# A two-layer GELU network on one core: the x sums placed earlier, the w1 forms of block 1 spread out, a w1 ring with places given out as they come free, and twice the warm-up products

## The chip, the core and the metric

The kernel runs on one core of a Trainium2 chip. The core has five engines that work side by side, each through its own queue and in the order of the program: TensorE (PE in the profile; its weight loads are listed apart as PEld), VectorE (DVE), ScalarE (ACT), GpSimd (POOL) and SyncE (SP). POOL and SP are used here mostly to issue DMA transfers; each issues its transfers in program order, and a transfer whose inputs are not ready holds up all that stand behind it in that queue. Matrix products land in PSUM, which has eight banks; the other engines read them from there.

The metric is the device time of one execution in microseconds (us); less is better. The median of three runs of the kernel before is 904.36 us (903.43 to 904.62).

## The reference

```python
# x: 16 x 512 x 768, w1: 768 x 3072, b1: 3072, w2: 3072 x 768, all float32
y = np.matmul(x, w1) + b1
y = 0.5 * y * (1.0 + erf(y / np.sqrt(2.0)))
return np.matmul(y, w2).astype(np.float32)
```

So 8192 rows of x go through a 768 to 3072 layer with bias and GELU, and then through a 3072 to 768 layer.

## The kernel before

**Pairs.** The 8192 rows are taken in eleven pairs (`pairs`), p = 0 to 10. Each pair is two halves of 384 rows (`HW`), the last one two halves of 256. x is loaded as bf16 by DMA through two buffers (`xb`), turned by a DMA transpose into `xt`, and multiplied as bf16. Hidden units are handled in 24 chunks of 128 (`HC`); chunk j and chunk 12+j belong together (`HP` = 12).

**Layer 1, plain.** Pair 0, and the first three j of pair 1 (`PLAIN` = 3), use ordinary products: `plain` (line 382 for its matmul) runs six matmuls of 128x384 for one chunk and one half, then ACT applies GELU (line 136) into `g`. `first` (line 445) is the same for the first three chunks of pair 0 while x is still coming in, 128 rows at a time.

**Layer 1, seven products.** Everywhere else `product1` (line 147) makes a 2x2 block of results (two halves of rows by chunks j and 12+j) from seven products P1 to P7 instead of eight, each three matmuls. Their x operands are the raw quarters of `xt` and four sums of them in `xft`, made by `sum_x(k, w)`, k = 0 to 3, one DVE instruction each; P1 needs sum 0, P7 needs sum 3. Their w1 operands are seven *forms* per j (raw quarters and sums of them), made once by `make_w1`: one ACT copy and four DVE instructions into a staging area (`stage`: parts of the tiles `ot`, `ev`, `xft` and `st`, whichever is out of use), and a DMA that writes them to DRAM (`w1f`). From there each pair loads them again, one j at a time, through a ring of five places (`RING`, `SLOT`) in `w1t`. The ring lies over the raw w1, so a place can be filled only when all raw w1 under it has been used. `load_slot(idx)` issues the load number idx from the SP queue; it is called by P3, the last user of a place, for the load five further on.

In pair 1 and later the products are interleaved: step s runs P1 and P7 of its j, P5 of the j before, P2, P3 of the j before, P4 and P6, 21 matmuls. After P2 and P6 `fill(s)` may put one sum of the second layer into the DVE queue.

**Layer 2, fifteen products.** The 768 rows of a pair make two groups G0 and G1 of three row tiles each (pair 10 has one group and a remainder). For a group, a 3x3 block of `g` times a 3x2 block of w2 is made from fifteen products M0 to M14, each eight matmuls (line 221). Their left operands are raw blocks of `g` or sums made on DVE by `gsum` (lines 109 and 112; into `st`, or in place in `g`), their right operands are sums of w2 made once by `make_w2`. Several products accumulate one after the other in the same PSUM bank (`BANK`): bank A takes M4, M12, M10, M11 in this order, bank B takes M13, M1, M9, M0, bank C M14 and M2, bank D M8 and M3. After every product `finish2` reads the bank: the first use is an ACT copy into an output tile `ot` (line 102), M7, M6 and the rest add on DVE (line 109). So a product waits until DVE has read its bank for the product before it. The `ot` tile has four places; a finished row tile is sent to DRAM by the POOL queue (`store`).

`rest(G, m, after)` runs product m, its `finish2`, and then the listed extra work. For G0 and G1 the order is: the six products on raw blocks (M14, M8, M4, M7, M6, M13), then `middle` (M12, M2, M1, M5, M3, M10, M9, M11), then M0. `middle` puts the sum for M5 after M12, the two for M9 after M2 and the two for M0 after M1; `extra(n)` follows product n of `middle`, n = 0 to 7. Between M11 and M0 of G1 `ahead` runs P1 and P7 of the next pair's first j.

All instructions are kept in program order on each engine (`tc.keep_in_program_order`), so what the Python text issues first is also first in the queue. The lines that decide the order around the change:

```python
            rest(G1, "M14", gsums(G1, "M1"))
            rest(G1, "M8", gsums(G1, "M3b"))
            rest(G1, "M4", gsums(G1, "M10b"))
            rest(G1, "M7", [form_w1] if p == 0 else ())
...
                return [lambda: sum_x(n - 4, nxt[1])] if 4 <= n < 8 else []
            middle(G1, extra)
            if p > 0:
                ahead(p + 1)
            rest(G1, "M0")
```

**Start.** Before pair 0 the kernel runs products on a zeroed tile, `busy(8)` and, after the first x tile has been turned, `busy(5)` (line 394, 128x512 each); nothing reads their results. `turn_x0` (line 411) transposes the first x tiles on PE.

## Time and profile before

| what | us |
|---|---|
| median of three runs (lowest, highest) | 904.36 (903.43, 904.62) |
| the profiled execution: its own time | 905.5 |
| its span, first to last instruction | 903.7 |
| PE busy | 878.2 (97% of the span), 5507 matmuls |
| DVE busy | 574.7 (64%) |
| ACT busy | 397.6 (44%) |
| POOL busy | 83.7 (9%) |
| mean granted clock of TensorE | 0.992 |

The profile page gives, for one execution, the busy time of each engine, the chain of work that ended last, and groups of instructions with what ended the idle time before them. The trace behind it can be asked for a timeline (instructions in order of time, equal ones merged, with the idle time before each in square brackets and what released it), for the waits (who waited for whom, total, times, longest), and for windows (busy time of each engine in given stretches, the granted TensorE clock, the share of the DMA engines in use). Matmuls overlap by their pipeline: a 128x384 one is listed with 320 to 326 ns, but 64 in a row from 81.31 to 91.70 us are 0.1624 us apart. An idle time of PE in the listing therefore understates by 0.16 us how late a matmul starts.

### The profile page before, as it was taken

The numbers are of one execution on the slowest core, as the hardware profiler recorded it, in microseconds if no ns is written. First come the engines' busy times: TensorE is split into PE (matmuls) and PEld (weight loads), VectorE is DVE, ScalarE is ACT, GpSimd is POOL, SyncE is SP. The second block draws the span as 40 slices with busy tenths as digits, with TensorE's granted clock in tenths as the row PEclk, the third lists the DMA queues.
The fourth block names the chain that finished last, engine by engine and source line by source line (L and its number), as shares of the span: only waits on it lengthen the run. The fifth ranks groups of instructions, "written<-read, shape, count | busy, mean of one in ns | idle before, by whom it ended". The sixth has DMA issues, their size and how long they took to land.

```text
span 903.7 us, 14021 instructions
## 1 busy us (share of the span) xinstructions
PE 878.2 (97%) x5507; PEld 536.0 (59%) x5507; DVE 574.7 (64%) x1068; ACT 397.6 (44%) x790; POOL 83.7 (9%) x152
## 2 busy tenths in 40 slices
PE   8998989999999999999999999999999999999998
PEld 6665546656655665566566566655665665666774
DVE  1687756675765776566667656675765766566654
ACT  2642277137415722761473177137415712751560
POOL 6201100110011011001101000110010011000000
PEclk8999989999999999999999999999999999999999
DMA  9996596736646682666467366736646682663521
GB/s 166 207 249 131 189 340 207 147 97 215 178 90 183 201 171 77 206 197 120 139 207 165 100 192 217 136 105 211 175 88 188 211 163 75 216 191 76 190 78 70
DMA packets 89303, 148.30 MB, mean 164 GB/s; under 512 B 50812, under 2 KB 68500, under 8 KB 89236
## 3 DMA queue, kind: packets, MB, share of 16 engines
q1 hardware_dynamic: 65156, 99.02, 37.2%
q0 software_dynamic: 24080, 48.37, 24.1%
q8 instruction: 43, 0.70, 0.3%
q14 instruction: 24, 0.20, 0.1%
HBM read 124.56 MB, written 33.42 MB: 175 GB/s over the span
## 4 chain that ended last, share of the span: by engine, by line
PE 85%; DVE 10%; DMA 3%; issue 1%; ACT 1%; POOL 0%; DVEq 0%; ACTq 0%; SPq 0%; POOLq 0%
PE ps L147 41%; PE ps L221 36%; PE ps L382 5%; DVE ot L109 4%; DVE xft L109 1%; DVE st L112 1%; DMA w1f<-st 1%; DVE st L109 1%; PE ps L445 1%; DMA w1t<-in_w_dram 1%; PE ps L631 1%; DVE xft L112 1%; DVE g L112 1%; DVE g L109 1%; DMA out_dram<-ot 1%
## 5 line engine op out<-in xcount | busy, mean ns | idle before, releaser
L147 PEld LDWEIGHTS <-w1t 128*128 128x128 bf16 x2457 | 240.2, 98 | 158.1 <-issue 12.2
L147 PE MATMUL ps<-xft,w1t 128*128 128x384 bf16 (+1 forms) x1404 | 263.4, 320 | 8.3 <-DVE xft L109 8.3
L136 ACT ACTIVATE g<-ps,b1t 128x384 bf16<-128x384 f32 (+1 forms) x411 | 222.3, 570 | 88.0 <-PE ps L147 67.3
L221 PE MATMUL ps<-w2t,g 128*128 128x384 bf16 x1512 | 257.5, 326 | 1.3 <-DVE ot L109 1.3
L109 DVE TENSOR_TENSOR ot<-ot,ps 128x384 f32<-128x384 f32 x231 | 123.9, 550 | 136.8 <-ACT ot L102 100.1
L221 PEld LDWEIGHTS <-g 128*128 128x128 bf16 x1512 | 147.9, 98 | 98.9 <-issue 1.5
L147 PE MATMUL ps<-xt,w1t 128*128 128x384 bf16 (+1 forms) x1053 | 205.0, 320 | 0.7 <-DVE ps L112 0.5
L221 PE MATMUL ps<-w2t,st 128*128 128x384 bf16 x1008 | 171.0, 326 | 1.4 <-DVE st L109 0.8
L102 ACT COPY ot<-ps 128x384 f32<-128x384 f32 x128 | 58.0, 485 | 238.2 <-PE ps L221 181.7
L221 PEld LDWEIGHTS <-st 128*128 128x128 bf16 x1008 | 98.4, 98 | 67.4 <-DVE st L109 1.2
L102 ACT COPY ps<-ps 128x384 f32<-128x384 f32 (+1 forms) x117 | 52.9, 452 | 134.6 <-PE ps L147 134.4
L112 DVE TENSOR_TENSOR ev<-ps,ev 128x384 f32<-128x384 f32 (+1 forms) x117 | 63.6, 544 | 72.7 <-PE ps L147 72.0
L112 DVE TENSOR_TENSOR ps<-ps,ev 128x384 f32<-128x384 f32 (+1 forms) x117 | 64.7, 553 | 44.9 <-PE ps L147 42.9
L104 DVE COPY ev<-ps 128x384 f32<-128x384 f32 (+1 forms) x117 | 63.4, 542 | 32.1 <-PE ps L147 32.1
L79 POOL DMA_DIRECT2D xb<-in_x_dram x58 | 31.2, 542 | 487.2 <-DMA xt<-xb 485.1
L136 ACT ACTIVATE g<-ev,b1t 128x384 bf16<-128x384 f32 (+1 forms) x117 | 70.9, 606 | 11.6 <-DVE ev L112 11.5
L112 DVE TENSOR_TENSOR st<-g 128x1024 bf16<-128x1024 bf16 x107 | 72.9, 682 | 0.0
L112 DVE TENSOR_TENSOR g<-g 128x1024 bf16<-128x1024 bf16 x84 | 57.4, 683 | 0.1
L79 POOL DMA_DIRECT2D out_dram<-ot x60 | 32.6, 543 | 242.7 <-DVE ot L109 237.2
L382 PE MATMUL ps<-xt,w1t 128*128 128x384 bf16 x252 | 43.6, 335 | 6.1 <-ACT g L136 6.1
L382 PEld LDWEIGHTS <-w1t 128*128 128x128 bf16 x252 | 25.3, 100 | 23.7 <-issue 8.4
L109 DVE TENSOR_TENSOR st<-st,g 128x1024 bf16<-128x1024 bf16 x42 | 28.9, 688 | 0.7
(62 smaller groups left out, 237.4 us busy)
## 6 DMA issues: line engine op xcount, KB each, us to landing
w1t<-w1f SPq DMA_DIRECT2D x117, 672.0 KB, 4.3
out_dram<-ot POOLq DMA_DIRECT2D x60, 384.0 KB, 2.7
xb<-in_x_dram POOLq DMA_DIRECT2D x58, 192.0 KB, 3.9
w2t<-in_w_dram POOLq DMA_DIRECT2D x8, 576.0 KB, 22.5
w1t<-in_w_dram POOLq DMA_DIRECT2D x5, 576.0 KB, 21.2
w1f<-st SPq DMA_DIRECT2D x4, 672.0 KB, 9.2
w1f<-ot POOLq DMA_DIRECT2D x2, 672.0 KB, 19.6
w1f<-ot SPq DMA_DIRECT2D x2, 672.0 KB, 6.4
```

The source lines that it names most:

```text
L79: inorder(queue.dma_start(out=out, in_=in_))
L102: inorder(nc.scalar.copy(out=dst, in_=src))
L104: inorder(nc.vector.tensor_copy(out=dst, in_=src))
L109: inorder(nc.vector.tensor_tensor(out=dst, in0=a, in1=b, op=ALU.add))
L112: inorder(nc.vector.tensor_tensor(out=dst, in0=a, in1=b, op=ALU.subtract))
L136: inorder(nc.scalar.activation(out=g[:, place_h(hc), half, :w], in_=src, func=ACTF.Gelu, bias=b1t[:, hc:hc + 1], scale=sign))
L147: inorder(nc.tensor.matmul(out=ps[:, :w], lhsT=forms[:, W1F[m], kc, :], rhs=moving1(m, kc, w), start=(kc == 0 and m in ("P1", "P7")), stop ...
L221: inorder(nc.tensor.matmul(out=ps[:, :NB], lhsT=lhs[:, c, :], rhs=w2t[:, c, WF[m], :], start=(m in OPENS and c == 0), stop=(c == QC - 1), ...
L382: inorder(nc.tensor.matmul(out=py[:, :HW], lhsT=lhs[:, kc, (j % 3) * P:(j % 3 + 1) * P], rhs=xt[:, kc, half, :], start=(kc == 0), stop=(kc ...
L445: inorder(nc.tensor.matmul(out=opened[hc][:, c0:c0 + P], lhsT=w1_group(0)[:, kc, hc * P:(hc + 1) * P], rhs=xt[:, kc, half, c0:c0 + P], sta ...
L631: inorder(nc.tensor.matmul(out=ps[:, :NB], lhsT=lhs[:, c, :], rhs=w2t[:, c, WF[f], :], start=(f == terms[0][0] and c == 0), stop=(f == ter ...
```

## The change

Eight things are done, all in one file:

1. `sum_x` 0 to 3 for the next pair follow M12, M2, M1 and M5 of G1's `middle` (n = 0 to 3), where they followed M3, M10, M9 and M11 (n = 4 to 7).
2. In every pair the G1 sums M1, M3b and M10b follow M4, M7 and M6, where they followed M14, M8 and M4.
3. In pair 0 the G0 sums M1, M3b and M10b are issued ahead of the raw products, where they came after them; the five `MIDDLE` sums of G1 follow G0's M9 and M11 and G1's M14, M8 and M4, where they followed G0's M5, M3, M10, M9 and M11. The two w1 forms that pair 0 makes in G1 follow M13 and M10 (they followed M7 and M9).
4. Block 1 (pair 1) made six w1 forms and the four x sums ahead of its twelve plain products. Now forms 6, 7 and 8 come ahead of the first, second and third chunk's two plain products, the x sums behind forms 6 and 7, and forms 9, 10 and 11 are made in two halves each from `fill` in the steps s = 0, 1 and 4.
5. The staging areas of forms 8 to 11 are the two halves of `ot` in the order upper, lower, upper, lower (they were lower, upper, and the two parts of `st`).
6. The w1 ring keeps a table `where` of the place of each load. A place is given out when it comes free: places 2, 3 and 4 when the raw w1 under them has been formed, places 0 and 1 when forms 9 to 11 are done too, and from then on by P3, which passes its own place to the next load number. Before, load idx always went to place (idx + 2) mod 5, and P3 of a step issued the load five further on.
7. `raw` forms count as used once their second half has been issued (`formed`).
8. `busy(5)` becomes `busy(10)`.

```diff
@@ -113,12 +113,15 @@
 
     total = (len(pairs) - 1) * HP - PLAIN
 
+    where = {}
+
     def slot(idx):
-        s = ((idx + FIRST) % RING) * SLOT
-        return w1t[:, s:s + SLOT]
-
-    def load_slot(idx):
+        return w1t[:, where[idx] * SLOT:(where[idx] + 1) * SLOT]
+
+    def fill_slot(k):
+        idx = len(where)
         if idx < total:
+            where[idx] = k
             dma(nc.sync, out=slot(idx), in_=w1f[(idx + PLAIN) % HP, :, :])
 
     def place_h(hc):
@@ -162,7 +165,7 @@
         elif m == "P4":
             gelu1(HP + j, 0, ps, w, 1.0)
         elif m == "P3":
-            load_slot((p - 1) * HP + j - PLAIN + RING)
+            fill_slot(where[(p - 1) * HP + j - PLAIN])
             gelu1(j, 0, ps, w, 1.0)
         elif m == "P5":
             gelu1(j, 1, u, w, -1.0)
@@ -339,40 +342,46 @@
 
     made = 0
     stage = ((otf, 0), (otf, N * 4), (evf, 0), (xftf, 0), (evf, 0), (xftf, 0),
-             (stf, 0), (stf, SLOT), (otf, 0), (otf, N * 4), (stf, 0), (stf, SLOT))
+             (stf, 0), (stf, SLOT), (otf, N * 4), (otf, 0), (otf, N * 4), (otf, 0))
 
     def make_w1():
         nonlocal made
-        j = (made + PLAIN) % HP
+        n = made
+        made += 1
+        j = (n + PLAIN) % HP
         a = raw(j)
-        area, o = stage[made]
-        queue = nc.gpsimd if made < 4 else nc.sync
-        made += 1
+        area, o = stage[n]
         s = area[:, o:o + SLOT].rearrange("p (f kc c) -> p f kc c", f=7, kc=KH)
         copy("act", s[:, 0:2], a[:, 1:3])
-        add(s[:, 2], a[:, 1], a[:, 2])
-        add(s[:, 3:5], a[:, 0:4:2], a[:, 1:4:2])
-        sub(s[:, 5], a[:, 2], a[:, 0])
-        sub(s[:, 6], a[:, 1], a[:, 3])
-        dma(queue, out=w1f[j], in_=area[:, o:o + SLOT])
-
-    nload = 0
-
-    def load_raw_slots(plain_done=0):
-        nonlocal nload
-        while nload < RING:
-            k = (nload + FIRST) % RING
+
+        def one():
+            add(s[:, 2], a[:, 1], a[:, 2])
+            add(s[:, 3:5], a[:, 0:4:2], a[:, 1:4:2])
+
+        def two():
+            sub(s[:, 5], a[:, 2], a[:, 0])
+            sub(s[:, 6], a[:, 1], a[:, 3])
+            dma(nc.gpsimd if n < 4 else nc.sync, out=w1f[j], in_=area[:, o:o + SLOT])
+            formed.add(j)
+
+        return one, two
+
+    formed = set()
+    ready = [(k + FIRST) % RING for k in range(RING)]
+
+    def free_slots(plain_done=0):
+        while ready:
+            k = ready[0]
             need = {j for j in range(HP) if HOME[j // 3] is not None
                     and HOME[j // 3] < (k + 1) * SLOT and HOME[j // 3] + 2 * GRP > k * SLOT}
-            have = {(PLAIN + n) % HP for n in range(made)}
-            if not need <= have or any(plain_done <= j < PLAIN for j in need):
+            if not need <= formed or any(plain_done <= j < PLAIN for j in need):
                 break
-            load_slot(nload)
-            nload += 1
+            fill_slot(ready.pop(0))
 
     def form_w1(plain_done=0):
-        make_w1()
-        load_raw_slots(plain_done)
+        for f in make_w1():
+            f()
+        free_slots(plain_done)
 
     def plain(hc, half):
         py = bank()
@@ -462,7 +471,7 @@
     tb = bank()
     inorder(nc.tensor.transpose(out=tb[:, :HC], in_=b1s, identity=ident32[:HC, :HC]))
     copy("act", b1t[:], tb[:, :HC])
-    busy(5)
+    busy(10)
     first(0)
     turn_x0(1, "dve")
     for n in range(2, 6):
@@ -478,13 +487,13 @@
             plain(hc, 1)
         if gi == 3:
             for _ in range(3):
-                make_w1()
+                form_w1()
             make_w2(2, 4)
             for G in blk:
                 for m in EARLY:
                     gsum(G, m)
         if gi == 5:
-            make_w1()
+            form_w1()
             for m in MIDDLE:
                 gsum(blk[0], m)
             make_w2(4, 6)
@@ -518,27 +527,42 @@
         if p > 0:
             js = list(range(PLAIN if p == 1 else 0, HP))
             last = len(js) - 1
+            more = []
             if p == 1:
                 hcs = [hc for j in range(PLAIN) for hc in (j, HP + j)]
-                form_w1()
-                form_w1()
-                for k in range(4):
-                    sum_x(k, w)
-                for _ in range(4):
-                    form_w1()
-                for hc in hcs:
+                for n, hc in enumerate(hcs):
+                    if n < 3:
+                        form_w1()
+                    if n < 2:
+                        sum_x(2 * n, w)
+                        sum_x(2 * n + 1, w)
                     plain(hc, 0)
-                    if hc == hcs[-1]:
+                    if n == len(hcs) - 1:
                         ahead(p)
                     plain(hc, 1)
-                load_raw_slots(PLAIN)
+                free_slots(PLAIN)
+                more = [0, 1, 4]
 
             both = (G0, G1) if full else (G0,)
             todo = {QH: [], 2 * QH: []}
             todo[QH] = [f for G in both for f in gsums(G, *EARLY)]
             todo[2 * QH] = [f for G in both for f in gsums(G, *MIDDLE)]
 
+            halves = []
+
             def fill(s):
+                if s in more and not halves:
+                    more.remove(s)
+                    halves.extend(make_w1())
+                    halves.append(None)
+                if halves and halves[0] is None:
+                    halves.clear()
+                elif halves:
+                    halves.pop(0)()
+                    if len(halves) == 1:
+                        halves.clear()
+                        free_slots(PLAIN)
+                    return
                 for first_j in (QH, 2 * QH):
                     if 0 <= s <= last and js[s] > first_j and todo[first_j]:
                         todo[first_j].pop(0)()
@@ -582,37 +606,40 @@
                 f()
         else:
             raws = ("M4", "M14", "M13", "M8", "M7", "M6")
+            for m in ("M1", "M3b", "M10b"):
+                gsum(G0, m)
             for c in range(QC - 1):
                 for m in raws:
                     part2(G0, m, (c,))
             for m in raws:
                 part2(G0, m, (QC - 1,))
                 finish2(G0, m)
-            for m in ("M1", "M3b", "M10b"):
-                gsum(G0, m)
 
         if nxt is not None:
             prepare_x(*nxt)
 
-        if p == 0:
-            mid = gsums(G1, *MIDDLE)
-            middle(G0, lambda n: mid[n - 3:n - 2] if 3 <= n < 8 else [])
-        else:
-            middle(G0, lambda n: [])
+        mid = gsums(G1, *MIDDLE) if p == 0 else []
+
+        def take(n):
+            r = mid[:n]
+            del mid[:n]
+            return r
+
+        middle(G0, lambda n: take(1) if n >= 6 else [])
         rest(G0, "M0")
 
         if full:
-            rest(G1, "M14", gsums(G1, "M1"))
-            rest(G1, "M8", gsums(G1, "M3b"))
-            rest(G1, "M4", gsums(G1, "M10b"))
-            rest(G1, "M7", [form_w1] if p == 0 else ())
-            rest(G1, "M6")
-            rest(G1, "M13")
+            rest(G1, "M14", take(1))
+            rest(G1, "M8", take(1))
+            rest(G1, "M4", take(1) + gsums(G1, "M1"))
+            rest(G1, "M7", gsums(G1, "M3b"))
+            rest(G1, "M6", gsums(G1, "M10b"))
+            rest(G1, "M13", [form_w1] if p == 0 else [])
 
             def extra(n):
                 if p == 0:
-                    return [form_w1] if n == 6 else []
-                return [lambda: sum_x(n - 4, nxt[1])] if 4 <= n < 8 else []
+                    return [form_w1] if n == 5 else []
+                return [lambda: sum_x(n, nxt[1])] if n < 4 else []
             middle(G1, extra)
             if p > 0:
                 ahead(p + 1)
```

## The prediction

> **What bounds the kernel now.** I read the page's busy times and chain first, then PE's waits, then the timeline and windows around each.
>
> ```profile
> PE 878.2 (97%) x5507; PEld 536.0 (59%) x5507; DVE 574.7 (64%) x1068; ACT 397.6 (44%) x790; POOL 83.7 (9%) x152
> PE 85%; DVE 10%; DMA 3%; issue 1%; ACT 1%; POOL 0%; DVEq 0%; ACTq 0%; SPq 0%; POOLq 0%
> PE ps L147 <- DVE xft L109: 8.3, 9, 0.9
> PE ps L382 <- ACT g L136: 6.1, 1, 6.1
> ```
>
> PE is the bound; time is won or lost only where PE starts late or its clock is down. Nine waits stand before P7 (L147 on xft: sum 3 comes late), one stands in block 1 (L382). The timeline has the rest: 0.34, 0.80 and 1.27 us in G0 of pair 0, 3.09 at the start. The end of pair 2 stands for all nine places:
>
> ```profile
> 263.14 1.02 DVE L109 TENSOR_TENSOR ot<-ot,ps 128x384 f32<-128x384 f32 x2 [6.00 <-ACT ot L102]
> 270.56 0.75 DVE L112 TENSOR_TENSOR xft<-xt 128x1152 bf16<-128x1152 bf16 x1
> 271.23 0.54 DVE L109 TENSOR_TENSOR ot<-ot,ps 128x384 f32<-128x384 f32 x1
> 271.69 0.75 DVE L109 TENSOR_TENSOR xft<-xt 128x1152 bf16<-128x1152 bf16 x1
> ...
> 262.77 5.36 PE L221 MATMUL ps<-w2t,st 128*128 128x384 bf16 x32 [0.23 <-ACT ot L102]
> 271.87 1.46 PE L221 MATMUL ps<-w2t,g 128*128 128x384 bf16 x8
> 274.76 0.65 PE L147 MATMUL ps<-xft,w1t 128*128 128x384 bf16 x3 [0.94 <-DVE xft L109]
> ```
>
> The DVE row at 271.23 is M10's add, over at 271.77. The PE row at 271.87 is M11, which accumulates in the same bank A and must wait for that add: the margin is 0.1 us. DVE is busy without a pause from 264.80 to 274.70. M7's add (263.14) had waited 6.00 us for ACT, and ACT for an output store (47.8 us in 10 waits over the kernel).
>
> For the clock, windows of 3.41 us on the grid on which the trace records it:
>
> ```profile
> 5.27:8.68 3.41, 1.55 (x9) 0.54 (x6) 0.56 (x1) 0.18 (x1) 2.58 (x5) 1.00 1.14 168
> 8.68:12.10 3.42, 2.20 (x21) 2.20 (x22) 0.00 (x0) 0.00 (x0) 1.74 (x3) 0.50 1.16 204
> ...
> 114.50:117.91 3.41, 0.44 (x2) 0.26 (x2) 2.46 (x8) 1.80 (x4) 0.00 (x0) 0.50 1.06 383
> 117.91:121.32 3.41, 3.41 (x13) 1.57 (x11) 0.00 (x0) 3.28 (x7) 0.00 (x0) 0.50 1.01 399
> ...
> 271.51:274.92 3.41, 2.47 (x17) 1.37 (x14) 3.19 (x6) 0.46 (x1) 0.54 (x1) 1.00 0.29 115
> 274.92:278.33 3.41, 3.41 (x23) 2.05 (x21) 1.61 (x3) 0.61 (x2) 0.74 (x2) 1.00 0.29 115
> ```
>
> First number after the comma is PE busy; the third from the right is the granted clock. A window with 1.86 us of PE idle is followed by half clock; one with 0.94 is not. A full window at half clock brings it back.
>
> **The change part by part**, in the profiled execution's own terms (905.5 us: span 903.7 and 1.8 around it; the median of the runs is 1.1 lower).
>
> *x sums and G1 sums moved, pairs 1 to 9.* Spacings on DVE from the rows above and between: add 0.465, g sum 0.61 (0.72 where it needs the one just before), x sum 0.67. From M7's add to the end of M10's add stood fifteen instructions; now twenty: M3b and M10b move in behind the late M7's add (they ran in the 6 us pause before), and x sums 1, 2 and 3 move ahead of M10's add. In a row: M7, M3b, M6, M10b 2.16; M12's add, M5's sum, x sum 1.745; M2's add, two M9 sums, x sum 2.465; M1's add, two M0 sums, x sum 2.455; M5's two adds, x sum 1.60; M3's add 0.465; M10's add 0.55 to its end. With t the start of M7's add after the start of M12, M10's add ends at max(t + 2.16, 1.47) + 9.28 (1.47: M12's own add cannot come sooner). M11's own place is 7 x 1.30 = 9.10. From the same two rows of each pair, t in pairs 1 to 9 is 0.29, 0.36, -1.32, -0.18, 0.13, 0.06, -0.52, 0.36, -1.89, so with 0.06 from DVE's end to PE's start M11 comes late by 2.69, 2.77, 1.71, 2.22, 2.53, 2.46, 1.88, 2.77 and 0.91 (pair 9: the sums of the short last pair cost 0.55): +19.9. What goes: P7's lateness, 0.94 + 0.16 for the overlap of matmuls = 1.10 eight times and 0.95: -9.8. M0's sums, M9 and M0's bank are ready earlier than M11 lets PE reach them. Net +10.2. DVE has no pause left in which this could hide. Bounds: ACT never late, 1.71 in eight pairs, +4.8; ACT as late as in pair 2 everywhere, 2.77, +13.3. The sums' own inputs are there: in pair 1 the last transpose lands at 179.6, and sum 0 is now wanted at 184. The output stores on POOL go out up to 4 us later; the next use of their tiles is 40 us on.
>
> *Pair 0, G0.* M1, M3b and M10b run on DVE from 65.9 to 67.7, under the raw products (until 69.29). M11, which started at 81.31, falls into its place 9.10 after M12's 69.29, 78.39: -2.9. M10's add then ends 0.08 ahead of M11, so up to 0.5 may come back. In G1 the five sums, M1, M3b, M10b and the two forms stand between adds; counted through with the same spacings, no product waits, with margins of 0.1 to 0.6.
>
> *Block 1.* ACT's form copy waited for the last output store, the GELUs behind it kept their banks, and PE stood:
>
> ```profile
> 111.73 1.56 ACT L102 COPY ot<-w1t 128x768 bf16<-128x768 bf16 x2 [9.90 <-DMA out_dram<-ot]
> 117.47 4.96 PE L382 MATMUL ps<-xt,w1t 128*128 128x384 bf16 x18 [6.11 <-ACT g L136]
> ```
>
> Form 8 now uses the half of ot that is sent first, and form 9 comes 12 us later, so PE does not stand: -6.3 (6.11 + 0.16). The x sums wait for form 5's write to leave xft; it goes out two DVE adds and form 6 earlier, about the time it needs (3.1 us alone in the row at 91.72). The 18 matmuls behind it took 4.80 us to the next product, at full clock 2.9: -1.9. What is late next: SP's queue. Loads 1 and 2 stand behind form 8's write; that is issued about 107.8, and three more writes, two output stores and two x loads are ahead of it. From 105 to 133 the DMA engines were full and a 0.69 MB transfer took 1.7 us; counted so, load 1 lands about 115.4, and the second j's P1 wants it at 114.1: +1.3 (0 to 3). Then steps 3 to 6 have only three places: P3 of a step ends, and 2 + 7 products later (4.39 us) the load it frees must be there. Between 131 and 155 us these loads took 3.8 to 4.2 us: they just fit. At 5.0 to 7.3 us (the loads from 113 to 129, in the crowd) each would be up to 3 late; I take +0.3 in all, being nearer to the calm rows, since of the writes only two remain then. This also holds the ACT copies (0.83) in steps 0, 1 and 4. Block 1: -6.6.
>
> *busy(10).* Five matmuls of 0.22 us fit in the 3.09 us wait for w1. PE's idle becomes 2.0 us. If the clock then stays up, the 128x128 products from 9.90 take 0.056 us each, not 0.107; counted through with the copies (0.56, 0.80), the first chunks end 2.1 us sooner, and nothing later holds that up (PE waits for no w1 load between 20 and 61). If it drops: 0. On the grid of this execution the idle splits 0.78 + 1.22, but the grid lies anew in each execution. I take half: -1.0.
>
> *The clock behind the new waits.* A window at half clock loses 1.7 us of work. Eight new waits are 1.7 to 2.8 us long. Where on the grid they fall is chance: for a wait g and a limit h on the idle time of a window, the share of positions that drop is (3.41 + g - 2h)/3.41. With h = 1.87 (what dropped) that gives 4.4 drops of eight, +7.5; with h = 0.94 (what held) nearly eight, +13.4; none, if the drop at 8.68 had another cause, 0. Between the first two I take 6: +10.2.
>
> The Trainium skill, page "TensorE: Matmul & The Clock Gate", section "HAM oscillation — how this bites in real kernels", has the rule that PE must not idle longer than about 3.4 us, a whole window. By it the new waits would leave the clock alone, and the sum below would be -0.3 in place of +9.9. The trace disagrees so far: the 3.09 us wait at the start was enough.
>
> Sum: 10.2 - 2.9 - 6.6 - 1.0 + 10.2 = +9.9, so 915.4 on the scale of the profile, 914 on that of the median.
>
> **The rivals.**
>
> *The clock holds.* The mechanism: only a window with far more idle than 1.9 us drops the clock. For it: one row alone (8.68) speaks against, at the start, after a cold stretch. Against it: the grid's first window after warm-up had 45% busy and fell at once. Then the sum is -0.3, or -1.4 with the start held: 903 to 904, not slower. It decides as soon as fewer than two of the nine waits drop the clock. The Trainium skill's rule above would give this case.
>
> *The ring starves.* Writes of forms 9 to 11 sit in the same SP queue as loads 3 to 8, so loads take 5 to 7 us and steps 3 to 6 wait 1 to 2 us each, load 1 comes 3 late: +8 on top, 922. For it: the 6.0 us loads of 113 to 129. Against: only one write falls between two loads.
>
> *M11 does not wait.* The x sums then simply take P7's waits away: -9.8 - 2.9 - 6.6 - 1.0 = -20.3, 884. It needs DVE to be 2.2 us further on at M10's add in the mean, which no row offers; even with ACT never late 1.71 remain.
>
> That the sums would not really move is no case: DVE runs in program order.
>
> **How the numbers follow.** Forecast 914: 0.60. Clock holds, 903 to 904: 0.18. Ring starves, 922: 0.16. M11 does not wait, 884: 0.06. A change under 0.2% (1.8 us) can't be told from none. Faster: the last case and a quarter of the second, 0.11; same: the half of the second and a little of the forecast, 0.11; slower 0.78. The range goes from the second case to half of the third: 902.5 to 919; the forecast's own is 907 to 918.
>
> **What would show it.** Right: PE waits before L221 on DVE ot, about nine of 0.8 to 2.6 us; no PE wait on xft, none of L382 on ACT; no idle in G0 of pair 0; half clock in windows after M11; one short PE wait on w1t in block 1. Wrong: M11 starts right behind M9; the clock stays at 1.00 behind waits of 2 us; steps 3 to 6 wait for w1t.

## The result, and the profile after

The changed kernel takes 910.77 us (median of 8 runs, 906.95 to 913.71), the kernel before 904.13 us (902.71 to 904.67, 8 runs): a ratio of 1.0074, 95% interval 1.0053 to 1.0095. It is slower by 6.6 us; forecast were 9.6 (914), range 902.5 to 919. The profiled execution took 911.75 us, span 910.0, so the sum of the prediction (+9.9 on the span) is set against +6.3.

The page of the changed kernel, busy times and chain: PE is still the bound, and it is busy for as long as before (878.2 then). The time is in PE's waits and its clock.

```profile
PE 879.7 (97%) x5512; PEld 535.3 (59%) x5512; DVE 573.8 (63%) x1068; ACT 398.5 (44%) x790; POOL 83.6 (9%) x152
PE 82%; DVE 10%; DMA 4%; issue 2%; ACT 1%; POOL 0%; DVEq 0%; SPq 0%; ACTq 0%; POOLq 0%
```

The waits of the changed kernel (engine, tile and line, what it waited for; total us, times, longest). Lines have moved: L147 is L150, L221 is L224, L382 is L391, L136 is L139. The two lines that led before, P7 on xft (8.3 in nine) and the plain product on ACT (6.1), are gone. In their place stand M11's bank (14.5, of which 14.2 in pairs 1 to 9) and the ring (5.2). ACT's waits for output stores fell from 47.8 us to 30.1.

```profile
ACT ot L102 <- DMA out_dram<-ot: 30.1, 9, 4.6
PE ps L224 <- DVE ot L109: 14.5, 10, 2.1
PE ps L150 <- DMA w1t<-w1f: 5.2, 3, 2.5
PE ps L454 <- DMA w1t<-in_w_dram: 2.4, 1, 2.4
```

The timeline of the changed kernel, in order of time: the end of pair 0, block 1, and the end of pair 2 (the counterpart of the rows shown of before).

```profile
89.68 1.63 ACT L102 COPY ot<-ps 128x384 f32<-128x384 f32 x4 [4.61 <-DMA out_dram<-ot]
90.21 4.06 PE L224 MATMUL ps<-w2t,st 128*128 128x384 bf16 x24 [1.79 <-ACT ot L102]
95.19 1.47 PE L224 MATMUL ps<-w2t,st 128*128 128x384 bf16 x8 [0.92 <-DVE st L109]
...
120.00 0.66 PE L150 MATMUL ps<-xft,w1t 128*128 128x384 bf16 x3 [2.53 <-DMA w1t<-w1f]
133.46 1.15 PE L150 MATMUL ps<-xft,w1t 128*128 128x384 bf16 x6 [0.87 <-DMA w1t<-w1f]
145.67 1.15 PE L150 MATMUL ps<-xft,w1t 128*128 128x384 bf16 x6 [1.80 <-DMA w1t<-w1f]
...
271.66 0.75 DVE L109 TENSOR_TENSOR xft<-xft,xt 128x1152 bf16<-128x1152 bf16 x1
272.32 1.47 DVE L109 TENSOR_TENSOR ot<-ot,ps 128x384 f32<-128x384 f32 x3
...
273.39 1.46 PE L224 MATMUL ps<-w2t,g 128*128 128x384 bf16 x8 [1.61 <-DVE ot L109]
274.68 1.14 PE L150 MATMUL ps<-xft,w1t 128*128 128x384 bf16 x6
```

The x sums, the last of them at 271.66, now stand ahead of M10's add (the second of the three that begin at 272.32; it ends at 273.33). M11 starts 0.06 later, at 273.39, 10.88 after M12 in place of 9.10: late by 1.78. P1 and P7 follow it without a wait.

Windows of the changed kernel, two of 4 us and the others of 3.41 us on the grid of the clock: after the comma PE busy, third from the right the granted clock. In the windows of 3.41 us idle is 3.41 less the busy time. Behind the rows with 2.53 and 2.06 idle the next window has half clock; behind the one with 1.62 it has not. The rows from 105 to 117 show the DMA engines (second from the right) full while the ring's first loads are on their way.

```profile
105.00:109.00 4.00, 4.00 (x26) 2.40 (x25) 3.97 (x10) 3.44 (x7) 1.35 (x3) 1.00 0.95 318
...
113.00:117.00 4.00, 4.00 (x27) 2.38 (x26) 0.56 (x1) 2.25 (x5) 0.00 (x0) 1.00 1.04 408
...
117.33:120.74 3.41, 0.88 (x6) 0.48 (x6) 1.04 (x3) 0.99 (x2) 0.00 (x0) 1.00 0.64 260
120.74:124.15 3.41, 3.41 (x13) 1.59 (x12) 1.56 (x4) 1.85 (x4) 0.00 (x0) 0.50 0.23 96
...
270.91:274.32 3.41, 1.79 (x12) 0.97 (x10) 2.89 (x6) 0.00 (x0) 0.54 (x1) 1.00 0.03 13
274.32:277.74 3.42, 3.42 (x23) 2.05 (x21) 1.69 (x4) 0.46 (x1) 0.54 (x1) 1.00 0.55 217
516.69:520.10 3.41, 1.35 (x10) 0.70 (x8) 2.99 (x6) 0.00 (x0) 0.54 (x1) 1.00 0.00 0
520.10:523.51 3.41, 3.41 (x12) 1.56 (x11) 0.90 (x2) 0.46 (x1) 0.54 (x1) 0.50 0.39 157
```

Where the time went, from the starts of the same PE products in the two profiled executions (first w2 product, M12 of G0, M14 of G1, first plain product of block 1, first product out of the ring, M14 of pair 1, the end):

| stretch | forecast | measured |
|---|---|---|
| start | -1.0 | -0.5 |
| pair 0, G0 | -2.9 | -2.9 |
| pair 0, G1 | 0 | +3.7 |
| block 1, up to the ring's first product | -8.2 | -8.2 |
| block 1, the steps on the ring | +1.6 | +7.4 |
| pairs 1 to 9: M11 late | +19.9 | +15.7 |
| pairs 1 to 9: P7's waits gone | -9.8 | -9.6 |
| clock behind M11 | +10.2 | +1.7 |
| rest | 0 | -1.0 |
| sum | +9.9 | +6.3 |

Of the rest, 0.6 are two small waits of before (262.77 and 871.81) that are shorter or gone.

### The profile page after: what moved, and what is told of

Read it like the earlier page. It is cut to its first block, busy times and chain, and to the rows that moved or that the text cites. A ratio compares the mean times of both kernels' runs of the same rounds, so it can differ in the third digit from the quotient of the medians.

```text
span 910.0 us, 14047 instructions
## 1 busy us (share of the span) xinstructions
PE 879.7 (97%) x5512; PEld 535.3 (59%) x5512; DVE 573.8 (63%) x1068; ACT 398.5 (44%) x790; POOL 83.6 (9%) x152
## 4 chain that ended last, share of the span: by engine, by line
PE 82%; DVE 10%; DMA 4%; issue 2%; ACT 1%; POOL 0%; DVEq 0%; SPq 0%; ACTq 0%; POOLq 0%
PE ps L150 40%; PE ps L224 35%; PE ps L391 5%; DVE ot L109 3%; DMA w1t<-w1f 2%; DVE st L109 1%; DVE xft L112 1%; DVE xft L109 1%; DMA out_dram<-ot 1%; DVE st L112 1%; DMA st<-in_x_dram 1%; PE ps L658 1%; DVE g L109 1%; DVE g L112 1%; PE ps L454 1%
## 5 line engine op out<-in xcount | busy, mean ns | idle before, releaser
L150 PEld LDWEIGHTS <-w1t 128*128 128x128 bf16 x2457 | 240.8, 98 | 155.8 <-DMA w1t<-w1f 6.4
L224 PE MATMUL ps<-w2t,g 128*128 128x384 bf16 x1512 | 258.4, 327 | 14.5 <-DVE ot L109 14.5
L150 PE MATMUL ps<-xft,w1t 128*128 128x384 bf16 (+1 forms) x1404 | 264.0, 322 | 5.2 <-DMA w1t<-w1f 5.2
L139 ACT ACTIVATE g<-ps,b1t 128x384 bf16<-128x384 f32 (+1 forms) x411 | 223.3, 570 | 92.0 <-PE ps L150 57.9
L224 PEld LDWEIGHTS <-g 128*128 128x128 bf16 x1512 | 148.1, 98 | 114.3 <-issue 17.7
L150 PE MATMUL ps<-xt,w1t 128*128 128x384 bf16 (+1 forms) x1053 | 205.8, 321 | 0.4
L224 PE MATMUL ps<-w2t,st 128*128 128x384 bf16 x1008 | 170.8, 326 | 2.7 <-ACT ot L102 1.8
L224 PEld LDWEIGHTS <-st 128*128 128x128 bf16 x1008 | 98.5, 98 | 68.3 <-issue 2.0
L139 ACT ACTIVATE g<-ev,b1t 128x384 bf16<-128x384 f32 (+1 forms) x117 | 70.9, 606 | 11.7 <-DVE ev L112 11.7
L112 DVE TENSOR_TENSOR g<-g 128x1024 bf16<-128x1024 bf16 x84 | 57.4, 683 | 0.1
L391 PE MATMUL ps<-xt,w1t 128*128 128x384 bf16 x252 | 41.6, 326 | 0.0
L391 PEld LDWEIGHTS <-w1t 128*128 128x128 bf16 x252 | 24.6, 98 | 16.2
L109 DVE TENSOR_TENSOR g<-g 128x1024 bf16<-128x1024 bf16 x42 | 28.9, 687 | 0.8
```

Of the source, the lines that this page charges most:

```text
L109: inorder(nc.vector.tensor_tensor(out=dst, in0=a, in1=b, op=ALU.add))
L112: inorder(nc.vector.tensor_tensor(out=dst, in0=a, in1=b, op=ALU.subtract))
L139: inorder(nc.scalar.activation(out=g[:, place_h(hc), half, :w], in_=src, func=ACTF.Gelu, bias=b1t[:, hc:hc + 1], scale=sign))
L150: inorder(nc.tensor.matmul(out=ps[:, :w], lhsT=forms[:, W1F[m], kc, :], rhs=moving1(m, kc, w), start=(kc == 0 and m in ("P1", "P7")), stop ...
L224: inorder(nc.tensor.matmul(out=ps[:, :NB], lhsT=lhs[:, c, :], rhs=w2t[:, c, WF[m], :], start=(m in OPENS and c == 0), stop=(c == QC - 1), ...
L391: inorder(nc.tensor.matmul(out=py[:, :HW], lhsT=lhs[:, kc, (j % 3) * P:(j % 3 + 1) * P], rhs=xt[:, kc, half, :], start=(kc == 0), stop=(kc ...
```

## The experiments

The theory after the result: over pairs 1 to 9 the place of the x sums alone costs; the clock falls only behind windows with about 2 us of idle; pair 0 and block 1 gain what was forecast up to a point, and give most of it back further on. The rivals: the moved sums for M3 and M10 are what makes M11 late; the ring's waits come from SP's queue; the start's lower clock has another cause than idle time.

### The x sums alone

```diff
# the kernel before
-                return [lambda: sum_x(n - 4, nxt[1])] if 4 <= n < 8 else []
+                return [lambda: sum_x(n, nxt[1])] if n < 4 else []
```

> The kernel before with the x sums alone moved forward (after products 0 to 3 of G1's middle). Theory (three x sums stand ahead of M10's add in DVE's queue, and M11 waits for that add): M11 comes late by about 1.8 us in pairs 1 to 8 and 1.0 in pair 9, P7 no longer by 1.1; net +5 to +6 us, about 910, and a spread of some us between executions when a wait falls into one clock window. Rival (the sums M3b and M10b behind the late M7 add are what makes M11 late): M11 stays in its place, P7's lateness is gone, about 895.

Measured 910.01 us (908.70 to 910.62, 5 runs) beside 905.14 for the kernel before: 1.0052 (1.0040 to 1.0064). This one line alone costs 4.9 us, of the 6.6 of the whole change. The timeline of this kernel has M11 in pair 2 late by the same 1.78:

```profile
271.48 1.47 DVE L109 TENSOR_TENSOR ot<-ot,ps 128x384 f32<-128x384 f32 x3
...
272.54 1.46 PE L221 MATMUL ps<-w2t,g 128*128 128x384 bf16 x8 [1.62 <-DVE ot L109]
```

It is 1.78 in pairs 1 to 8 alike, also in pair 5, where M7's add came at +0.36, as late as the prediction ever had it. Without M3's and M10's sums behind it, that lateness is absorbed, and M12's own add sets the chain. So the rival falls: the moved sums cost nothing but in the pairs where ACT is late (0.45 in pair 5 of the changed kernel).

### The x sums back

The changed kernel with the x sums at n = 4 to 7, as before (the diff above, the other way round).

> The changed kernel with only the x sums put back behind M3, M10, M9 and M11. Theory: M11's waits (15.7 us of lateness in nine pairs) go, P7's 9.6 come back, and the clock drop behind M11 goes: 910.8 - 6 to - 8, so 903 to 905; M11 late by less than 0.8 where M7's add comes late. What else the change did nets to about nothing. Rival (the rest of the change, ring and pair 0, carries the loss): 908 or more.

Measured 902.27 us (901.60 to 902.31): 0.9967 (0.9956 to 0.9979), a little under what was expected and faster than the kernel before. The waits of this kernel: P7's are back, M11's have gone but for one of 0.55 us in pair 5, where ACT is late, and the ring waits 3.6 us.

```profile
PE ps L150 <- DVE xft L109: 8.4, 9, 1.0
PE ps L150 <- DMA w1t<-w1f: 3.6, 3, 2.4
```

Everything else in the change is thus worth about -2.9 us, and the nine pairs decide its sign.

The two runs do not add up: 4.9 and -2.9 make 2.0, and the whole change has 6.6. About 2.2 of the 4.6 between them can be read from the clock. On the kernel before, the mean granted clock of the runs is the same with the x sums moved (0.993) as without (0.994); on the changed kernel it is 0.996 in place of 0.998, some 1.3 windows of half clock at 1.7 us. Another 0.45 is pair 5's later M11. The 2 us left are within the intervals of the three ratios and stay open.

### Pair 0's order alone

The kernel before with the hunks on pair 0 alone (M1, M3b and M10b of G0 ahead of the raw products, the five sums of G1 at n = 6, 7 and behind M14, M8, M4, G1's M1, M3b and M10b behind M4, M7 and M6, the two forms behind M13 and M10).

> The kernel before with only pair 0's order of the changed kernel (G0's M1, M3b and M10b ahead of its raw products, the five G1 sums and the two forms later). Theory: G0 is 2.9 us shorter, its three output stores leave earlier, meet the last x loads and transposes on the DMA engines and land 5 to 8 us after issue instead of 2.6 to 3.4, ACT's copy of M4 in G1 waits for one of them and M12 comes 1 to 2 us late; G1 gives back 2 to 4 us, net within 1 us of before, 903 to 905. Rival (the late stores of the changed kernel were chance): G1 gives nothing back, 901.

Measured 902.27 us (899.15 to 904.95, 10 runs) beside 905.14: 0.9973 (0.9961 to 0.9985). These -2.9 are more than the 1 us at most that was expected, and less than the rival's -4. In its profile G0 gained 2.9 and G1 gave 1.5 back, where 2 to 4 were expected; M12 did not wait for ACT there, only M5, M11 and M0 came late (0.66, 0.06 and 0.28 in the listing). Of G0's three output stores, issued from 79.0 to 82.0 here and from 80.5 to 85.0 before, the DMA view shows how long they took (KB each, median us from issue to landing; first the kernel before, then this one, then the changed kernel):

```profile
out_dram<-ot POOLq DMA_DIRECT2D x3, 384.0 KB, 2.6
...
xt<-xb SPq DMA_TRANSPOSE x2, 3.3
```

```profile
out_dram<-ot POOLq DMA_DIRECT2D x3, 384.0 KB, 5.9
...
xt<-xb SPq DMA_TRANSPOSE x2, 6.2
```

```profile
out_dram<-ot POOLq DMA_DIRECT2D x3, 384.0 KB, 6.8
...
xt<-xb SPq DMA_TRANSPOSE x2, 7.8
```

The third store of before landed at 87.54. Issued about 3 us earlier, it landed at 87.84 here and at 89.58 in the changed kernel. ACT's copy for M4 needs its tile, M7's add needs ACT, and G1's sums stand behind that add; so G1 starts earlier and its middle does not. In the five other profiles with this order the third store lands between 86.2 and 88.2 and G1 gives back 0.6 to 3.8. The order of the sums is not what makes the stores slow. With block 1 alone and with `busy(17)`, two runs below that have pair 0's order of before, the start is 3.7 and 2.3 us earlier in the profile; there the stores took 6.3 and 4.7 us in the median, and the third landed at 87.58 and 87.31. In eleven of the twelve profiles the third store lands between 86.2 and 88.3, wherever between 80.0 and 85.7 it was issued. That stores which leave early are slow because the last x loads and transposes run beside them is read from the rows; no run takes the transposes away.

### A longer wait

The changed kernel with x sum 0 made twice, so that M10's add comes one sum (0.67 us) later. The second sum writes the same values.

```diff
-                return [lambda: sum_x(n, nxt[1])] if n < 4 else []
+                return [lambda: sum_x(n, nxt[1])] * (2 if n == 0 else 1) if n < 4 else []
```

> The changed kernel with x sum 0 of each pair made twice, one more DVE instruction of 0.67 us ahead of M10's add. Theory on the clock (a window of 3.41 us with more than about 1.7 us of PE idle is followed by one at half clock): M11 late by 2.45 instead of 1.78 us, +6 us, and half clock behind about six of the nine waits, 1.7 us each: 920 to 928, widely spread between executions. Rival (waits this short leave the clock alone): +6 us only, 917, with a small spread.

Measured 922.72 us (921.05 to 925.91): 1.0196 (1.0180 to 1.0213), some 12 us over the changed kernel for nine sums of 0.67 = 6.0 us. In its profile M11 is late by 24.5 us in sum, 8.8 more than in the changed kernel: 0.79 more in pairs 2, 3, 7 and 8, and 1.35 to 1.68 more in pairs 1, 4 and 6, where M7's add came late too. Most of the rest is the clock: behind M11's waits it is down for five windows in place of one. Four of the six windows of this kernel with over 1.4 us of idle that hold one of M11's waits, in the order of time:

```profile
187.11:190.52 3.41, 1.39 (x9) 0.71 (x8) 3.38 (x7) 0.00 (x0) 0.00 (x0) 1.00 0.00 0
357.78:361.19 3.41, 1.76 (x11) 1.07 (x11) 2.33 (x6) 0.00 (x0) 0.54 (x1) 1.00 0.30 111
...
610.36:613.77 3.41, 1.49 (x10) 0.90 (x10) 2.33 (x5) 0.00 (x0) 0.54 (x1) 1.00 0.21 83
692.28:695.69 3.41, 1.00 (x7) 0.56 (x6) 2.93 (x6) 0.00 (x0) 0.54 (x1) 1.00 0.00 0
```

Idle is 2.02, 1.65, 1.92 and 2.41 us here, 2.97 and 2.10 in the two left out. Half clock followed 2.02, 2.10, 2.41 and 2.97, and neither 1.65 nor 1.92. So the clock does fall behind these waits, as forecast, though behind four of the nine and not six, and at a limit between 1.7 and 2.0 us of idle in one window: over the twelve profiles of this study every window at full clock with 2.02 or more was followed by half clock and none with 1.68 or less; between, 1.73 and 1.86 fell, and 1.76, 1.80, 1.84 and 1.92 held. (A window that is itself at half clock is another matter: the one at 8.68 in the kernel before, with 1.22 of idle, did not bring full clock back.) A wait of 1.62 can't reach that wherever it lies on the grid.

### The sums in DVE's pause

The changed kernel with all four x sums of pairs 1 to 9 behind M10's sum, in the pause in which DVE waits for ACT ahead of M7's add, and M1, M3b and M10b of G1 back at M14, M8 and M4 in these pairs. The expectations further on call this kernel e6_pause.

```diff
# the changed kernel, p > 0
-            rest(G1, "M14", take(1))
-            rest(G1, "M8", take(1))
-            rest(G1, "M4", take(1) + gsums(G1, "M1"))
-            rest(G1, "M7", gsums(G1, "M3b"))
-            rest(G1, "M6", gsums(G1, "M10b"))
+            rest(G1, "M14", gsums(G1, "M1"))
+            rest(G1, "M8", gsums(G1, "M3b"))
+            rest(G1, "M4", gsums(G1, "M10b") + [lambda k=k: sum_x(k, nxt[1]) for k in range(4)])
+            rest(G1, "M7")
+            rest(G1, "M6")
...
-                return [lambda: sum_x(n, nxt[1])] if n < 4 else []
+                return []
```

> The kernel after, with all four x sums of pairs 1 to 9 behind M10's sum in DVE's pause ahead of M7's add, and the sums for M1, M3 and M10 of G1 back behind M14, M8 and M4. Block 1, pair 0 and the start as after. Theory (what costs is only the place of the sums between M7's add and M10's add): M11 never waits, P7 never waits, M7's add still comes when ACT lets it, since the last transpose lands 6.3 to 8.5 us before M12, and seven sums (4.5 us) are done 1.5 us or more before M7's add. That is 9.6 us below the 902.3 with the sums behind M10's add: 892 to 893. Rival (the pause is not free: the x transposes come too late and hold M7's add and the whole chain): M12 or M11 waits by 0.5 us or more in most pairs, and the time is 897 or more.

Measured 892.18 us (891.43 to 893.26): 0.9859 (0.9846 to 0.9872), as expected. The timeline of this kernel at the end of pair 2:

```profile
254.82 0.76 DVE L109 TENSOR_TENSOR xft<-xt 128x1152 bf16<-128x1152 bf16 x1 [1.49 <-DMA xt<-xb]
...
256.41 0.76 DVE L109 TENSOR_TENSOR xft<-xft,xt 128x1152 bf16<-128x1152 bf16 x1
257.09 1.01 DVE L109 TENSOR_TENSOR ot<-ot,ps 128x384 f32<-128x384 f32 x2
...
267.01 1.46 PE L224 MATMUL ps<-w2t,g 128*128 128x384 bf16 x8
268.31 1.14 PE L150 MATMUL ps<-xft,w1t 128*128 128x384 bf16 x6
```

Sum 1 waits 1.49 us for the last transpose, so the sums end later than the expectation had them, at 257.17 and not 1.5 us ahead of M7's add. M7's add follows at once (257.09), 0.82 ahead of M12, which is early enough. M11 (267.01) starts 9.10 after M12 (257.91), P1 and P7 right behind. The prediction said that DVE has no pause left in which the sums could hide; that was true of the stretch behind M7's add, and the pause ahead of it was not asked.

### The sums in the pause, alone

```diff
# the kernel before
-            rest(G1, "M4", gsums(G1, "M10b"))
+            rest(G1, "M4", gsums(G1, "M10b") + ([lambda k=k: sum_x(k, nxt[1]) for k in range(4)] if p > 0 else []))
...
-                return [lambda: sum_x(n - 4, nxt[1])] if 4 <= n < 8 else []
+                return []
```

> The kernel before, with nothing changed but the place of the four x sums of pairs 1 to 9: behind M10's sum, in DVE's pause ahead of M7's add. Theory (the place of these sums alone decides over nine pairs): P7's nine waits go (8 x 1.10 and 0.79 = 9.6) and M11 doesn't wait, 895 to 896 beside the before's 904.9. Rival (the gain of e6_pause needs the other parts, since they release ACT's stores earlier): M7's add comes late, and the time is 899 or more.

Measured 895.00 us (894.92 to 897.01) beside 904.55: 0.9901 (0.9885 to 0.9917), -9.6 as expected. In its waits P7 on xft is gone, and of M11 on its bank 0.07 us is left, in pair 6: there sum 1 waited 4.72 us for the last transpose, until 582.13, M7's add came behind it, and M11 started 0.55 us late behind M12. So the pause suffices only while the transposes are in time. What remains is the start (3.5), pair 0 and block 1, of which two lines:

```profile
PE ps L382 <- ACT g L136: 5.9, 1, 5.9
PE ps L221 <- DVE ot L109: 1.3, 1, 1.3
```

### Block 1 alone

The kernel before with the ring's places, the forms' spread and their areas as in the changed kernel; the x sums, pair 0's sums and the start as before.

> The kernel before with the part on block 1 alone: ring with places given out as they come free, forms 6 to 11 spread, their areas as in the kernel after; the x sums and all of pair 0's sums and busy(5) as before. By the prediction's own term it takes 6.6 off: 898. Theory from the milestones of the kernel after and of the runs so far: the 6.1 us gap goes with the half clock behind it (-8.2 up to the first step) and the steps that follow give 5.5 to 7.4 back in three waits on w1t and a second half-clock window, in all -0.8 to -2.7: 902 to 904.

Measured 903.63 us (900.22 to 906.09, 12 runs) beside 904.55: 0.9990 (0.9977 to 1.0003). The forecast's -6.6 is not there. The profiled execution, at 900.22, is the fastest of the twelve; its first w1 columns came early, at 8.03. In it block 1 gains 8.15 up to the ring's first product and gives 5.35 back on the steps (4.5 of it the three waits below). This execution lost nothing to the clock behind the ring's first wait, since that wait fell across two windows; the changed kernel lost a window there. The timeline of PE in block 1:

```profile
117.23 0.66 PE L150 MATMUL ps<-xft,w1t 128*128 128x384 bf16 x3 [3.40 <-DMA w1t<-w1f]
125.67 1.15 PE L150 MATMUL ps<-xft,w1t 128*128 128x384 bf16 x6 [0.88 <-DMA w1t<-w1f]
139.97 1.15 PE L150 MATMUL ps<-xft,w1t 128*128 128x384 bf16 x6 [0.21 <-DMA w1t<-w1f]
```

### Form 11 earlier, and the forms' writes on another queue

Two runs on the kernel with the sums in the pause: `more = [0, 1, 2]` in place of `[0, 1, 4]`; and the writes of forms 9 to 11 on POOL's queue.

> As e6_pause, with form 11 at step 2 in place of step 4 of block 1, so that the nine last places of the ring come free two steps earlier. Theory (behind load 3 the steps wait because three places alone turn over): the waits on w1t after step 2 (0.97 and 0.25 in the run with the sums behind M10's add, 0.87 and 1.80 in the kernel after) go, 1 to 2.5 us below e6_pause; the wait of the first load (2.4) stays. Rival (the transfers themselves are slow, not the places): the waits move or stay, and the time is that of e6_pause within 0.6.

Measured 890.05 us (889.31 to 894.62): 0.9845 (0.9825 to 0.9865), the lowest median of this study, but its interval overlaps that of the sums in the pause (0.9846 to 0.9872): not settled. The waits on the ring are 2.33, 0.24 and 1.51 in place of 2.54, 0.94 and 1.19. The late wait (142.85 there) is gone; the three loads that form 11 lets go at once, issued within 1.7 us of each other, now come at 127 to 129 and took 6.9 to 8.8 us there. The wait stands at 130.89, for a load issued at 124.60 just ahead of them, which took 6.3 us (5.3 there). So neither expectation holds as written: places did come free earlier, and the burst of loads moved with them.

> As e6_pause, with the writes of forms 9 to 11 on POOL's queue and not on SP's. Rival (loads stand in SP's queue behind these writes): the waits after step 2 go, 1 us or more below e6_pause. Theory (the loads are issued when their places come free, the writes in the queue cost 0.3 us of issue each): the same time as e6_pause within 0.6.

Measured 892.63 us (888.75 to 893.01): 0.9854 (0.9836 to 0.9871), no gain. The waits on the ring of this kernel, and then the DMA issues of its stretch from 118 to 150 us (KB each, median us from issue to landing):

```profile
PE ps L150 <- DMA w1t<-w1f: 4.8, 3, 1.8
```

```profile
w1t<-w1f SPq DMA_DIRECT2D x11, 672.0 KB, 6.6
w1f<-ot POOLq DMA_DIRECT2D x3, 672.0 KB, 6.4
xb<-in_x_dram POOLq DMA_DIRECT2D x2, 192.0 KB, 13.1
```

The loads no longer stand behind the writes, and the waits are 4.8 us in place of 4.7: SP's order is not what makes them. The run was not clean. Two x loads on POOL's queue went out 23 us earlier than in the kernel with the writes on SP's queue (134.96 in place of 157.85) and met the ring's loads; M12 of pair 1 waited 2.52 us for ACT, which it does not there; and the clock did not fall behind the first wait on the ring, which was 1.81 in place of 2.54. So the equal time alone says little, and the reading rests on the waits.

### The start alone

The kernel before with `busy(17)` in place of `busy(5)`: twelve matmuls more, whose result nothing uses.

> The kernel before with busy(17) in place of busy(5), the start alone. Twelve more matmuls of 0.22 us fill 2.6 of the 3.09 us for which PE waits for the first w1 columns, so some 0.5 us of idle is left. Theory (idle time in a 3.41-us window lowers the clock, limit between 1.66 and 2.0 us): no half clock at 11.5, the 128x128 products take 0.056 us each and the start is 2.1 us shorter, about 903.0 beside the before's 905.1. Rival (the fall at 11.5 belongs to the cold start or to the short products, not to the idle time): half clock stays in that window, and the time stays at 905.1 within 0.5.

Measured 904.78 us (902.73 to 907.66, 12 runs) beside 904.87: 0.9999 (0.9987 to 1.0010). The profile shows the theory's mechanism and the time doesn't. In the profiled execution, which with 902.73 is one of the two fastest of the twelve, there is no half clock at the start, and the first w2 product comes 2.29 earlier. First the start of this kernel, then of the kernel before with the sums in the pause, then with block 1 alone, both with busy(5); the first w1 product waits in each:

```profile
5.75 3.84 PE L394 MATMUL ps<-st 128*128 128x512 bf16 x17
9.79 1.18 PE L445 MATMUL ps<-xt,w1t 128*128 128x128 bf16 x18 [0.20 <-DMA w1t<-in_w_dram]
```

```profile
10.57 1.67 PE L445 MATMUL ps<-xt,w1t 128*128 128x128 bf16 x14 [3.48 <-DMA w1t<-in_w_dram]
```

```profile
8.03 1.18 PE L454 MATMUL ps<-xt,w1t 128*128 128x128 bf16 x18 [0.69 <-DMA w1t<-in_w_dram]
```

The first w1 columns come at 8.03 in one execution and at 10.57 in another, with the same start. Where they come late, the filler saves a window's clock; where they come at 8.03, the 17 matmuls that end at 9.59 are 1.6 us in the way. The mean granted clock of the twelve runs is 0.996, beside 0.994 for the kernel before, which is about one half-clock window less; so 1.7 us were gained in most of them and lost again elsewhere. That they are lost to the 17 matmuls is argued, as only one of the runs was profiled. The row at 8.03 also shows that short products alone don't lower the clock: they ran at 0.066 us each (1.18 for 18), at full clock, behind 0.69 us of idle. So the rival's mechanism falls, though its time came true.

## Why the prediction was right, and where it was not

**M11's wait: right, one term a quarter too large.** The formula put the end of M10's add at max(t + 2.16, 1.47) + 9.28 after M12's start. In the changed kernel t, the start of M7's add, is -1.42, -1.49, -1.09, -0.77, -0.13, -1.35, -1.72, -1.27 and -1.89 in pairs 1 to 9. The formula then gives M11 late by 1.71 where t is under -0.69 (measured 1.78) and by 2.27 in pair 5 (measured 2.23). The mis-sized term is t: it was taken over from the rows of before (0.29, 0.36, -1.32 ...), while it follows the landing of an output store, which differs from execution to execution. With the bound "ACT never late" the net was forecast as +4.8; +6.1 was measured, +10.2 forecast. That the move of M3b and M10b matters only where ACT is late was in the formula, and the run with the x sums alone shows it.

**P7's waits gone: right** (-9.8 forecast, -9.6 measured), and the run with the x sums back shows them returning.

**The clock behind the new waits: wrong in size, the largest miss.** Forecast were six half-clock windows and +10.2, measured one and +1.7. The step that failed is the choice of six, between the count for h = 1.87 (what dropped) and that for 0.94 (what held), on waits that were taken too long. Seven waits came out at 1.62 and pair 9's at 0.82, under the limit of 1.7 to 2.0 that the runs show; only pair 5's, 2.06, dropped the clock. With h = 1.87 and these waits the prediction's own formula gives half a drop. As the waits would have been (1.7 to 2.8) more would have dropped: the run with one more sum shows four drops behind nine waits of 1.4 to 3.1 us. The smaller t and the higher limit took 8.5 us off together. By the prediction's own sign, fewer than two drops of nine, it was the case "clock holds" that came. It named the right behaviour for these waits but priced the rest too low, at 903 to 904: block 1 and pair 0 were given more than they had.

The Trainium skill, page "TensorE: Matmul & The Clock Gate", section "HAM oscillation — how this bites in real kernels", asks for no idle beyond about 3.4 us. The runs disagree: idle of 2.02 to 2.97 us within a window of 3.41 us, with PE busy at the rest of it, halved the clock of the next one in four windows of one execution.

**Pair 0: half right.** G0's -2.9 came as counted. What failed is "counted through with the same spacings, no product waits" for G1. The count leaves out what M7's add waits for, and that did not come earlier with G0: the add waits for ACT, ACT for the third output store, and that lands 8.1 us after issue in place of 2.6. M12 waited 1.79 for ACT, M5 0.92 and M0 0.28 for DVE, and 3.7 were given back. The prediction named output stores on POOL, but only the ones that would go later.

**Block 1: the gap right, the ring wrong.** PE's gap and the half clock behind it went (-8.15 for -8.2). Then "these loads took 3.8 to 4.2 us: they just fit" and +1.6 for the whole ring failed; +7.4 was measured. Loads 1 and 2 took 8.4 and 8.9 us from issue to landing, with the DMA engines full from 105 to 117; the 2.53 us wait behind them dropped the clock for a window (1.7). Load 4 took 5.2, and four loads that were issued within 4.3 us behind form 11's write took 7.7 in the median of the three whose landing the trace has (4.0 in the same stretch before). The rows are those of the changed kernel from 111 to 114 and from 138 to 143 us, and of the kernel before from 131 to 143:

```profile
w1t<-w1f SPq DMA_DIRECT2D x2, 672.0 KB, 8.7
```

```profile
w1t<-w1f SPq DMA_DIRECT2D x4, 672.0 KB, 7.7
```

```profile
w1t<-w1f SPq DMA_DIRECT2D x4, 672.0 KB, 4.0
```

The rival "the ring starves" said +8 on top with waits of 1 to 2 us in steps 3 to 6; +5.8 on top came, with three waits (2.53, 0.87 and 1.80) and one half-clock window. Its cause was taken to be SP's queue; the run with the writes on POOL speaks against that, and full DMA engines and loads issued together are what the traces show. Which of the two weighs more stays open. Alone, the part on block 1 is worth -0.9 us, within its interval of nothing.

**The start: right in the mechanism, unsure in the time.** The profile has -0.5; the clock was lowered in this execution as before. The run with busy(17) says that filling the wait gains nothing over many executions.

So the forecast's side came out by its mechanism, M11's wait. That the time came within 3.6 us of the sum is in part luck, errors against each other: the clock (-8.5) and M11 (-4.2) were taken too high, the ring (+5.8) and G1 of pair 0 (+3.7) too low.

## What to carry to other kernels

An add that frees an accumulation bank belongs ahead of work that is wanted later; before moving work forward in an in-order engine, look for the pause in which the engine already waits, and check that the inputs have landed by then. Here the same four sums cost 5 us ahead of the add, and gained 9.6 us in the pause before it. A transfer that goes out earlier meets other transfers: work moved up by 3 us gave back up to 3.7 through stores, and a ring relieved of one long gap gave back 5.4 to 7.4 through loads in a crowd.

## What the runs showed that was not expected

- The clock is lowered for a whole window of 3.41 us by the idle in the window before it, from 1.7 to 2.0 us on, not at one sharp value. So waits of 1.6 us cost only themselves, and of the nine of 1.4 to 3.1 us in the run with one sum more four were followed by half clock, at 1.7 us a window.
- In the changed kernel a pair takes 81.7 us, close to 24 windows of 3.413 (81.9): in pairs 1 to 4 the wait lies whole within one window, and with the x sums alone moved it does so in all eight full pairs; each held. Drops behind a wait of a repeating loop are thus not independent draws, as the prediction's share of positions took them.
- The same first load of w1 columns lands between 8.0 and 10.6 us in different executions of the same start.
- Loads of 672 KB that took 4.0 us (median) when issued 3.4 us apart took 7.7 and 8.7 when two to four were issued together with the DMA engines full. Stores of 384 KB that took 2.6 in the kernel before took 6.8 where they left earlier, beside the last two x transposes, and those took 7.8 in place of 3.3.
